# A two-layer hybrid decoder trunk on one core: the remainder of some weight slabs computed by an adding DMA in place of VectorE

## The chip, the cores and the metric

The kernel runs on one core of a Trainium2 chip. The metric is the device time of one execution in microseconds (us). Five engines matter: TensorE (PE in the profile, with PEld for its weight loads), VectorE (DVE), ScalarE (ACT), GpSimd (POOL) and SyncE (SP), which issues nearly all DMAs.

## The reference

The input, 512 tokens with 16 meta tokens ahead of them, goes through two layers of width 1024. Cut to what matters here:

```
for l in range(2):
    h = layer_norm(a * h + 0.5 * swiglu(h, ffn 0 of layer l))
    u = h @ w_in[l]                       # split into three mixers: RG-LRU, SSD, gated DeltaNet
    h = layer_norm(a * h + concat(mixers(u)) @ w_out[l])
    h = layer_norm(a * h + 0.5 * swiglu(h, ffn 1 of layer l))
```

Each SwiGLU has a gate, an up (1024x2816) and a down matrix (2816x1024). All weights and activations are f32.

## The kernel before

**Precision.** Every large product is made of three passes in a rounded f32 format (fp32r). A weight w is split into hi, which is w rounded, and lo = w - hi; the activations are split likewise. `gemm` sums hi*xhi, lo*xhi and hi*xlo.

**Slabs.** Weights come in slabs of 128x1024 elements (512 KB). `slab` (line 628) makes one ready. SP loads it into a raw tile `wr` (three buffers, `RAWS`). ScalarE rounds it into the hi half of a tile `wt` (six buffers, `TILES`). Then the remainder lo = raw - hi is computed either by GpSimd, in `PARTS` = 4 pieces of 128x256, or by VectorE in one instruction of 128x1024. The raw buffer is free once the remainder has been read out of it; the `wt` buffer is free after the last matmul of the slab.

**Streams.** The 528 tokens are two streams of 272 and 256. In the stretches before and after (the "shared" FFN parts) both streams use a slab once it is loaded. In the stretches between, the streams run apart: while one is in its mixer (long chains of small operations on all engines), the other fills TensorE with FFN work. There each slab is read by one stream alone. A slab of this kind has its fourth key `r` not None (FFN) or comes from `proj` or `out` of the mixer. Of the kernel's 484 slabs 168 are shared and 316 are read by one stream alone. `pools()` (line 648) takes POOL_SHARE = 0.7 of the latter for GpSimd. The remaining 95, and all shared slabs, take the VectorE branch. `weave` and `KNOTS` set how the two streams' units are interleaved.

**Order of the work.** Nothing is issued as it is written. A `Recorder` collects all operations with their data dependencies; `price` (line 121) gives each one a cost and, for DMAs and weight loads, a second figure `load`; `levels` computes from the end how much work hangs on each operation; `schedule` lists them engine by engine, in order of priority, and assigns the buffers; `issue` emits this order, and each engine works through its queue in order. `CHAINED` (line 44) names the tile tags for which the operation that ends the use of a buffer also inherits the urgency of the tile that will take this buffer next; before, these are the PSUM tiles `psg.g` and the weight tiles `wt.wt`. All instructions are issued from line 389, so the profile has nearly one line only, and groups are told apart by their tiles: `wr` raw slab, `wt` split slab, `g` PSUM of the large products, `c` PSUM of the mixers and norms, `acc` the residual sum, `fs`, `fh`, `ft`, `hid` FFN and convolution tiles, `d_*`, `db`, `lru`, `s_*` mixer tiles.

Of the kernel before, what the change touches and what calls it, by code (L numbers as in the profile page):

```python
# [12 lines left out]
ALU = mybir.AluOpType  # L13
# [27 lines left out]
KNOTS = ((0, 20), (18, 32), (30, 72), (59, 72), (69, 75), (72, 84), (72, 93), (82, 94), (88, 102), (89, 114), (93, 127), (95, 133), (108, 148), (108, 157), (114, 163), (117, 163), (117, 163), (117, 163), (117, 166), (132, 166))  # L41
FIRST = ("psg.g", "psc.c")
CFIRST = 1
CHAINED = ('psg.g', 'wt.wt')
WARM = 0.45
MARGIN = (20, 5, 5, 5, 0)
SPARE = dict(wr=99, db=99, lru=99, wt=99, mt=99, s2=99, g=99, c=3)
# [33 lines left out]
class Recorder:  # L81
# [39 lines left out]
    def price(self, eng, name, args, kw):  # L121

        a = [x for x in args if hasattr(x, "ap")]
        n = self.size(a[0])
        if name == "dma_start":
            b = n * a[0].ap[0][1] * 4
            return (1040 if eng == self.POOL else 475), b / 360.0
        if eng == self.PE:
            w, x = (a[1], a[2])
            fast = w.dtype == F32R  # L130
            c = (1 if fast else 2 if name == "transpose" else 4) / 2.4
            if self.region(a[0])[0] and self.size(w) <= 64:
                return self.PAIR, 55
            return self.size(x) * c + 2.5, self.size(w) * c
        wide = max(self.size(x) for x in a)
        psum = any(x.space == bass.MemoryType.PSUM for x in a)
        if eng == self.DVE:
            if name == "reciprocal":
                return 68 + 6.25 * n, 0
            if name in ("tensor_scalar", "tensor_copy", "memset") and not psum:  # L140
                return 68 + 0.52 * n, 0
            scalar = [x for x in a[1:] if self.size(x) == 1 < wide]
            return (127 if scalar else 68) + 1.042 * wide, 0
        if eng == self.ACT:
            extra = sum(93 for k in ("bias", "scale") if hasattr(kw.get(k), "ap"))
            return (51 if psum else 94) + 0.833 * wide + extra, 0
        if name in ("memset", "affine_select"):
            return 36 + 0.85 * n * (2 if name == "affine_select" else 1), 0
        return (120 + 3.33 * n if name == "tensor_copy" else 148 + 2.1 * n), 0
# [87 lines left out]
    def levels(self):  # L237
# [12 lines left out]
        for tag, sl in self.tags.items():  # L250
            tiles = [t for t in first if self.slot[t] is sl]
            if tag == "psg.g":
                for t, u in zip(tiles, tiles[1:]):
                    first[t].after.append((first[u], sum(o.cost for o in self.ops[first[t].seq:end[t].seq] if o.eng == self.PE and t in o.tiles)))
            if tag in CHAINED:
                done = sorted((end[t] for t in tiles), key=lambda op: op.seq)
# [142 lines left out]
class Trunk:  # L399
# [225 lines left out]
    def new_acc(self, u):  # L625
        self.acc[u] = self.tl(self.ap, [P, KD, 272], f"acc{u}")[:, :, :NTOK[u]]

    def slab(self, srcs, ncol, pool):

        nc = self.nc  # L630
        raw = self.tl(self.wr, [P, KD, P], "wr")[:, :, :ncol]
        t = self.tl(self.wt, [P, 2, KD, P], "wt", F32R)
        hi, lo = t[:, 0, :, :ncol], t[:, 1, :, :ncol]
        for c0, s in srcs:
            nc.sync.dma_start(raw[:, :, c0:c0 + s.shape[2]], s)
        nc.scalar.copy(hi, raw)
        if pool and self.pools():
            for k in range(0, KD, KD // PARTS):
                part = slice(k, k + KD // PARTS)
                nc.gpsimd.tensor_tensor(lo[:, part], raw[:, part], hi[:, part].bitcast(F32), ALU.subtract)  # L640
        else:
            nc.vector.tensor_tensor(lo, raw, hi.bitcast(F32), ALU.subtract)
        return hi, lo
# [999 lines left out]
```

## Time and profile before

| | us |
|---|---|
| three timed runs | 2479.98, 2482.42, 6374.14 (median 2482.42) |
| the profiled execution, whole | 2475.13 |
| its span, first to last instruction | 2472.2 |
| PE / DVE / ACT / POOL busy | 2303.2 / 1548.9 / 881.4 / 913.3 |

The time outside the span is 2.9 us. The third timed run stands far off the other two and plays no part in what follows. In the rows a window's numbers are the busy time of each engine and, in brackets, the count of its instructions; PEclk is the mean granted TensorE clock as a share of 2.4 GHz; the DMA share is that of the core's 16 DMA engines.

### The profile page before, as it was taken

Reading aid. Unit: us, or ns where it says so; the run is one execution under the profiler, and the core shown is the slowest. Engines: PE = TensorE matmul, PEld = TensorE weight load, DVE = VectorE, ACT = ScalarE, POOL = GpSimd, SP = SyncE. Lnnn points to the kernel's source line nnn. Section 1 sums busy time; section 2 is a strip of 40 time slices with the busy share of each in tenths; the row PEclk is TensorE's granted clock in tenths of the full one; section 3 lists DMA queues with packets and bytes.
Section 4 is the critical chain, followed back from the end, with each engine's and each line's share of the span. In section 5 each row is a group of like instructions: output and inputs, shape, how many; then the busy total and the mean of one; then the engine's idle time right before and its main releaser. Section 6 shows DMA issues by size and latency. Waiting matters only on the chain. (4 is left out here: it accounts for less than half of the span.)

```text
span 2472.2 us, 46955 instructions
## 1 busy us (share of the span) xinstructions
PE 2303.2 (93%) x18698; PEld 2199.2 (89%) x18698; DVE 1548.9 (63%) x3529; ACT 881.4 (36%) x1546; POOL 913.3 (37%) x1298
## 2 busy tenths in 40 slices
PE   8999998998888899999999999988889888999997
PEld 7999997886787899999999999978778778999997
DVE  6444468777877665444574444787788677654445
ACT  3222344342334354222242223533433344542222
POOL 4000566653554675000000006667365646740000
PEclk9999999897899899999999999989988879999999
DMA  5323454432341456232222334534234415653330
GB/s 147 98 78 102 125 151 148 124 86 66 100 128 46 145 163 187 95 95 86 79 76 84 97 93 145 165 111 134 62 86 124 118 34 166 179 164 91 94 95 34
DMA packets 426330, 271.98 MB, mean 110 GB/s; under 512 B 33420, under 2 KB 407920, under 8 KB 425856
## 3 DMA queue, kind: packets, MB, share of 16 engines
q1 hardware_dynamic: 425536, 268.83, 37.3%
q8 instruction: 146, 2.39, 0.4%
q0 software_dynamic: 576, 0.16, 0.1%
q14 instruction: 72, 0.59, 0.1%
HBM read 260.76 MB, written 8.19 MB: 109 GB/s over the span
## 5 line engine op out<-in xcount | busy, mean ns | idle before, releaser
L389 PE MATMUL g<-hh,wt 128*128 128x256 f32 (+1 forms) x7616 | 1073.2, 292 | 35.3 <-DVE fh L389 10.4
L389 PEld LDWEIGHTS g<-hh,wt 128*128 128x128 f32 x7616 | 995.2, 194 | 48.8 <-DVE fh L389 11.1
L389 POOL TENSOR_TENSOR wt<-wr,wt 128x256 fp32r<-128x256 f32 x884 | 699.8, 823 | 728.8 <-ACT wt L389 692.7
L389 ACT CAST wt<-wr 128x1024 fp32r<-128x1024 f32 x484 | 498.3, 1041 | 622.9 <-PE g L389 486.8
L389 PE MATMUL g<-hl,wt 128*128 128x256 f32 (+1 forms) x3808 | 568.0, 289 | 1.9 <-DVE hl L389 1.3
L389 PE MATMUL g<-hid,wt 128*128 128x256 f32 (+1 forms) x4224 | 541.8, 286 | 11.7 <-DVE acc L389 5.4
L389 PEld LDWEIGHTS g<-hid,wt 128*128 128x128 f32 x4224 | 524.0, 189 | 18.6 <-DVE acc L389 7.3
L389 PEld LDWEIGHTS g<-hl,wt 128*128 128x128 f32 x3808 | 507.0, 192 | 7.4 <-DVE hl L389 2.7
L389 DVE SCALAR_TENSOR_TENSOR acc<-g,acc 128x256 f32<-128x256 f32 (+1 forms) x608 | 255.7, 428 | 228.4 <-PE g L389 222.6
L389 DVE TENSOR_TENSOR wt<-wr,wt 128x1024 fp32r<-128x1024 f32 x263 | 339.3, 1301 | 93.0 <-ACT wt L389 91.2
L389 DVE SCALAR_TENSOR_TENSOR fs<-ft,g 128x272 f32<-128x272 f32 (+1 forms) x200 | 84.6, 424 | 176.4 <-ACT ft L389 175.6
L389 DVE TENSOR_TENSOR fh<-fs,g 128x256 f32<-128x256 f32 (+1 forms) x176 | 74.9, 426 | 173.1 <-PE g L389 172.6
L389 ACT ACTIVATE ft<-g 128x272 f32<-128x272 f32 (+1 forms) x208 | 80.8, 389 | 286.8 <-PE g L389 267.3
L389 ACT CAST hid<-fh 128x256 fp32r<-128x256 f32 (+1 forms) x176 | 71.9, 408 | 226.7 <-DVE fh L389 224.8
L389 POOL TENSOR_TENSOR ls<-ls,lq 128x256 f32<-128x256 f32 (+1 forms) x30 | 24.9, 829 | 268.8 <-ACT lq L389 268.5
L389 DVE TENSOR_TENSOR hid<-fh,hid 128x256 fp32r<-128x256 f32 (+1 forms) x176 | 87.0, 494 | 40.2 <-ACT hid L389 40.1
L389 POOL TENSOR_TENSOR wr<-wr,db 128x512 f32<-128x512 f32 x4 | 5.0, 1277 | 260.1 <-ACT wr L389 260.1
L389 DVE SCALAR_TENSOR_TENSOR fs<-fh,par,fs 128x272 f32<-128x272 f32 (+1 forms) x144 | 87.4, 609 | 20.1 <-ACT fh L389 11.3
L389 ACT ACTIVATE ft<-fs 128x272 f32<-128x272 f32 (+1 forms) x56 | 23.6, 425 | 82.1 <-DVE fs L389 77.8
L389 DVE SCALAR_TENSOR_TENSOR acc<-acc,par,c 128x256 f32<-128x256 f32 (+1 forms) x104 | 43.7, 482 | 8.7 <-PE c L389 8.7
L389 ACT ACTIVATE fs<-g,par 128x272 f32<-128x272 f32 (+1 forms) x48 | 25.1, 523 | 56.3 <-PE g L389 37.3
L389 ACT ACTIVATE lq<-acc 128x256 f32<-128x256 f32 (+1 forms) x84 | 34.6, 419 | 25.6 <-PE c L389 9.2
(306 smaller groups left out, 1741.2 us busy)
## 6 DMA issues: line engine op xcount, KB each, us to landing
wr<-in_ffn_w_gate_dram SPq DMA_DIRECT2D x120, 512.0 KB
wr<-in_ffn_w_up_dram SPq DMA_DIRECT2D x120, 512.0 KB
wr<-in_ffn_w_down_dram SPq DMA_DIRECT2D x120, 512.0 KB
wr<-in_w_in_dram SPq DMA_DIRECT2D x88, 512.0 KB
wr<-in_w_out_dram SPq DMA_DIRECT2D x32, 512.0 KB
res<-acc SPq DMA_DIRECT2D x2, 1088.0 KB
acc<-res SPq DMA_DIRECT2D x8, 272.0 KB
acc<-in_x_dram SPq DMA_DIRECT2D x4, 512.0 KB
```

The lines of the kernel that those rows point to most:

```text
L389: op.fn(*[on(x) for x in op.args], **{k: on(x) for k, x in op.kw.items()})
```

## The change

For a slab that one stream alone reads and that `pools()` does not give to GpSimd, ScalarE now writes the negated rounded weights into lo (`mul` by -1) and then hi, and a DMA issued from GpSimd's queue adds raw onto lo in place. VectorE's subtract of such a slab goes. Shared slabs and GpSimd's slabs are as before. `price` gets a cost for an adding DMA, 880 ns of its queue and twice a plain transfer's load, and `CHAINED` gets the raw tiles `wr.wr`; both enter the planned order of everything.

```diff
-CHAINED = ('psg.g', 'wt.wt')
+CHAINED = ('psg.g', 'wt.wt', 'wr.wr')
...
         if name == "dma_start":
             b = n * a[0].ap[0][1] * 4
+            if kw.get("accum_op") is not None:
+                return 880, 2 * b / 360.0
             return (1040 if eng == self.POOL else 475), b / 360.0
...
-    def slab(self, srcs, ncol, pool):
+    def slab(self, srcs, ncol, alone):
...
         for c0, s in srcs:
             nc.sync.dma_start(raw[:, :, c0:c0 + s.shape[2]], s)
+        if alone and not self.pools():
+            nc.scalar.mul(lo, raw, -1.0)
+            nc.scalar.copy(hi, raw)
+            nc.gpsimd.dma_start(lo, raw, accum_op=ALU.add)
+            return hi, lo
         nc.scalar.copy(hi, raw)
-        if pool and self.pools():
+        if alone:
             for k in range(0, KD, KD // PARTS):
                 part = slice(k, k + KD // PARTS)
                 nc.gpsimd.tensor_tensor(lo[:, part], raw[:, part], hi[:, part].bitcast(F32), ALU.subtract)
```

## Rows read from the trace of the kernel before

**Rows 1.** The page: busy time of each engine and share of the span.
```profile
PE 2303.2 (93%) x18698; PEld 2199.2 (89%) x18698; DVE 1548.9 (63%) x3529; ACT 881.4 (36%) x1546; POOL 913.3 (37%) x1298
```

**Rows 2.** Windows: two mixer stretches, two edges and a shared stretch, all instructions.
```profile
core 0: us, PE busy (x) PEld busy (x) DVE busy (x) ACT busy (x) POOL busy (x), PEclk, DMA share, GB/s
400.00:900.00 500.00, 439.43 (x3611) 397.30 (x3611) 385.37 (x1003) 204.82 (x396) 285.54 (x412) 0.90 0.37 105
900.00:1000.00 100.00, 98.14 (x796) 96.67 (x796) 52.37 (x94) 39.69 (x53) 54.60 (x71) 1.00 0.58 174
1600.00:2100.00 500.00, 434.68 (x3550) 389.71 (x3550) 372.91 (x1003) 196.78 (x385) 285.83 (x414) 0.88 0.38 107
2100.00:2180.00 80.00, 78.45 (x648) 77.14 (x646) 49.07 (x102) 39.82 (x62) 59.19 (x75) 1.00 0.56 165
...
1000.00:1500.00 500.00, 496.24 (x4027) 493.20 (x4026) 258.67 (x498) 142.63 (x242) 19.74 (x23) 1.00 0.29 87
```

**Rows 3.** Windows: the instructions on wt alone, in the two mixer stretches.
```profile
400.00:900.00 500.00, 313.77 (x2219) 292.43 (x2219) 35.29 (x28) 96.41 (x93) 210.00 (x259) 0.90 0.37 105
...
1600.00:2100.00 500.00, 302.29 (x2128) 279.92 (x2128) 35.11 (x27) 92.88 (x90) 204.86 (x252) 0.88 0.38 107
```

**Rows 4.** Groups of the whole span: the three operations that split a slab.
```profile
L389 POOL TENSOR_TENSOR wt<-wr,wt 128x256 fp32r<-128x256 f32 x884 | 699.8, 823 | 728.8 <-ACT wt L389 692.7
L389 ACT CAST wt<-wr 128x1024 fp32r<-128x1024 f32 x484 | 498.3, 1041 | 622.9 <-PE g L389 486.8
L389 DVE TENSOR_TENSOR wt<-wr,wt 128x1024 fp32r<-128x1024 f32 x263 | 339.3, 1301 | 93.0 <-ACT wt L389 91.2
```

**Rows 5.** The chain of waits, 1826 to 2088 us: shares, then three of its pieces.
```profile
by line: PE g L389 25.7%; PE c L389 20.0%; DVE fs L389 8.7%; DVE d_sq L389 5.3%; DVE l_h L389 3.9%; issue 3.3%; DVE acc L389 3.3%; DVE wt L389 2.9%; DVE db L389 2.7%; DVE d_ss L389 2.5%; DVE lru L389 2.5%; DVE d_t L389 2.0%; ACT wt L389 1.9
...
1881.66 4.29 POOL wt L389 x4
...
1928.80 1.13 DVE wt L389
...
1934.32 1.03 ACT wt L389
```

**Rows 6.** Windows: the instructions on wt alone, 1826 to 2088 us.
```profile
1826.00:2088.00 262.00, 156.68 (x1111) 146.55 (x1112) 17.11 (x13) 47.47 (x46) 106.69 (x128) 0.86 0.38 107
```

**Rows 7.** Waits of SP's queue and of ACT, 900 to 1000 us: us in total, times, longest.
```profile
SPq L389 <- POOL wt L389: 36.8, 16, 3.1
SPq L389 <- DVE wt L389: 15.8, 6, 6.8
...
ACT wt L389 <- PE g L389: 27.7, 9, 5.9
```

**Rows 8.** The chain of waits, one raw buffer's round in an edge: start, us, what.
```profile
2089.99 4.86 DMA wr<-in_ffn_w_gate_dram
...
2094.93 1.06 ACT wt L389
...
2096.06 3.13 POOL wt L389 x4
...
2156.55 3.60 DMA wr<-in_ffn_w_down_dram
```

**Rows 9.** The page: DMA queue of the loads; DMA issues on GpSimd's queue (KB, us to landing).
```profile
q1 hardware_dynamic: 425536, 268.83, 37.3%
...
fh<-in_ln_b_dram POOLq DMA_DIRECT2D x1, 24.0 KB, 6.6
...
fh<-in_ssd_dt_bias_dram POOLq DMA_DIRECT2D x1, 8.0 KB, 2.8
```

**Rows 10.** Timeline of POOL at the start: DMA issues, us each.
```profile
1.56 0.70 POOL L389 DMA_DIRECT2D fh<-in_ln_g_dram  x1
2.25 0.52 POOL L389 DMA_DIRECT2D fh<-in_ln_b_dram  x1
```

**Rows 11.** Waits of PE, 1500 to 2180 us: the three longest.
```profile
PE c L389 <- DVE db L389: 9.5, 7, 4.0
PE c L389 <- DVE lv L389: 5.6, 2, 4.9
PE c L389 <- DVE dt_g L389: 5.4, 2, 4.7
```

**Rows 12.** Tile wt on POOL, 320 to 1000 us: ns min/median/max.
```profile
L389 POOL TENSOR_TENSOR wt<-wr,wt x390: 250/741/2600, 319.0 to 973.8; 128x256 fp32r<-128x256 f32 x193, 128x32 fp32r<-128x32 f32 x2
```

## The prediction

> **What bounds the kernel now.** The page comes first: PE is busy for 93% of the span, no other engine for more than 63% [rows 1]. So time can only come out of PE's gaps and out of stretches where its clock is low, and the windows show where these are. In the shared stretch from 1000 to 1500 us PE is busy for 496 of 500 us at full clock; nothing is to be had there, and the change leaves its slabs alone. In the two mixer stretches (400 to 900 and 1600 to 2100 us) PE is busy for 439 and 435 of 500 us, so 61 + 65 = 126 us are gaps, and the mean clock is 0.90 and 0.88. Between the two levels, 1 and 0.5, that is a fifth to a quarter of the time at 1.2 GHz. DVE is at 77% and 75% there, the highest of the other engines [rows 2]. The list of PE's waits says the same: the longest are all on small DVE results of the mixers [rows 11]. Around the mixers lie four edges where one stream's FFN runs almost by itself (two stand in rows 2). There PE is at 98% and full clock, and the work that could run out is the supply of slabs: DMA share 0.56 to 0.58, and SP's queue waits most for POOL to release a raw buffer [rows 2, 7].
>
> **What goes.** 95 of the 263 DVE subtracts, each 1.30 us [rows 4]: 95 x 1.30 = 124 us of DVE. 28 + 27 = 55 of them lie in the mixer stretches [rows 3], where 55 x 1.3 = 72 us out of 758 us bring DVE from 76% to 69%. The other 40 lie in the edges, where DVE is half idle. What a subtract is worth is read from the chain of waits. From 1826 to 2088 us, 2.9% of 262 us = 7.6 us of the chain are DVE on wt [rows 5], and 13 such instructions ran there [rows 6]: 0.58 us of the 1.3 is on the chain, on average. 55 x 0.58 = 32 us. This supposes that no second chain is close behind; between nothing and the whole 72 us is possible, and I take 32, since it is read from the same stretch.
>
> **What comes, on ScalarE.** 95 multiplies of 128x1024. No such form stands in the trace; the nearest is the rounding copy of the same shape, 1.04 us [rows 4], so 99 us on an engine at 40% in the mixers. Below, it can't be shorter than nothing; above, twice the copy. I take 1.04. On the chain, ACT on wt holds 1.9% of 262 = 5.0 us for 46 copies [rows 5, 6], 0.11 us each: 55 x 0.11 = 6 us lost. (With the multiply first, hi comes 1.04 us later; the six wt buffers hide that, since ACT often waits for PE to free one of them [rows 7].)
>
> **What comes, on GpSimd's queue.** 95 DMA issues. The trace has small ones of 0.52 to 0.70 us [rows 10]; an adding one of 128 rows does not occur. I take 0.7 and, as ends, 0.5 and 3.1 (the four subtracts of a whole slab, rows 8). The queue is in order, so an issue that waits for ACT's multiply holds up the subtracts and mixer operations behind it, for up to one ACT operation of 1.04 us. POOL on wt has one piece of 4.3 us on that chain against 106.7 us busy [rows 5, 6], 4%: 55 x (0.7 + 1.04) x 4% = 4 us. The same rows count for the gain: with 32 - 6 - 4 = 22 us, the mixers get faster by 22.
>
> POOL's pieces take 0.74 us in the median and up to 2.6 [rows 12], so something on the core holds them up now and then. The Trainium skill (SBUF — State Buffer, section "Who interferes with whom") states that a VectorE instruction with two SBUF inputs blocks GpSimd's reads, and that a DMA issued from GpSimd is starved of its descriptors while VectorE runs in a two-port mode. By the first half POOL would gain where a subtract goes, by the second the new issues would stretch. No row tells these apart, and the sum holds neither.
>
> **What comes, on the DMA engines and the raw buffers.** A slab's remainder is now ready when the DMA has landed, and its raw buffer is held until then. That time is not in the trace. The loads move 268.8 MB in 37.3% of 2472 us, so 291 GB/s when all engines are busy [rows 9], and 512 KB take 1.8 us. Two reads for one write make it 3.6 at most, and the short fixed part of a DMA from GpSimd's queue is 2.8 us [rows 9]: 6.4 us from issue to landing. The ends are 3.6 us (a down slab's load, which has long rows as well, rows 8) and 6.6 + 2 x 4.86 = 16.3 us (the worst small DMA and two gate loads in a row, rows 8, 9). I take 6.4.
> The Trainium skill (Collectives: The Full Stack, "The bandwidth ceiling: the fold count and why AG ≠ RS ≠ AR") states that an add needs two source reads and so halves the rate of a copy, while the add itself costs nothing. No run here shows it; by it the data part would be the 3.6 us above.
>
> One round of a raw buffer now: load 4.86, copy 1.06, four subtracts 3.13, hand-overs 0.2, so 9.3 us with POOL [rows 8], and 4.86 + 1.06 + 1.30 + 0.2 = 7.4 with DVE. With 70% and 30%, over three buffers, a slab can come every (0.7 x 9.3 + 0.3 x 7.4) / 3 = 2.9 us. PE needs 24 matmuls per slab, 98.14 / 796 x 24 = 2.96 us [rows 2]: the supply just suffices. After the change the 30% take 4.86 + 1.06 + 0.7 + 6.4 + 0.2 = 13.2 us, and a slab comes every (0.7 x 9.3 + 0.3 x 13.2) / 3 = 3.5 us. In the mixer stretches that does no harm (500 us / 93 slabs = 5.4 us per slab, rows 3). The edges hold 316 - 183 = 133 slabs, 33 each; there 33 x 0.54 = 18 us are short, less the stock in the wt buffers (six, of which two are in use: 4 x 2.96 = 12 us). So 6 us per edge, 24 in all. The bounds are -6 us (PE's 2% of gaps over some 340 us of edges can't give more) and 4 x 18 = 72 us without stock. I take a third of the 24, 8 us, because the new CHAINED entry moves the operations that free a raw buffer forward; the trace shows no size for this.
>
> **The sum.** Against the profiled execution's 2475.1 us: -22 + 8 = -14, so 2461. The two near runs lie 5 to 7 us above that execution (2479.98 and the median 2482.42), so on the median's scale 2482.4 - 14 = 2468.
>
> **The rivals.**
> - VectorE is the bound of the mixers. Then all 72 us of subtracts come out, less 6 on ACT: 2482 - 66 = 2416. For it: DVE at 77%, PE's waits on DVE, and a clock that may rise when gaps close [rows 2, 11]. Against it: only 2.9% of the chain is DVE on wt [rows 5].
> - Nothing: the mixer's small operations form a second chain just behind, ACT and POOL take back what DVE gives, and the new order is as good as the old: 2480. For it: 'PE g' and 'PE c' hold 46% of the chain [rows 5].
> - The supply breaks in the edges, on the other side. The adding DMAs read and write what the loads' engines must carry: some 10 per 100 us x 3.6 us are 0.36 on top of a DMA share of 0.58, 0.94. If landings lengthen by a fifth (loads 5.8, adding DMAs 7.7), rounds are 10.2 and 15.5 us, a slab comes every 3.9 us, and 33 x 0.97 - 12 = 20 us are lost per edge, 80 in all: 2482 - 22 + 80 = 2540. It decides from 3.5 us per slab (18 us short, all of the mixers' gain gone), and passes 2% at 3.9. For it: supply and need are level now, 2.9 against 2.96. Against: the edges are only 30 to 35 slabs long, and the stock covers the first part.
>
> **How the numbers follow.** The forecast has 0.42, VectorE as the bound 0.24, nothing 0.11, the broken supply 0.23. Two per cent (50 us) is about what a measurement of this kernel can tell from no change. Faster by over 2%: 0.24. Within 2%: 0.42 + 0.11 = 0.53. Slower: 0.23. Cases of both signs hold weight, so the forecast's own range is 2445 to 2490; the range that holds 8 in 10 reaches from 2410 (all of DVE's 72 us) to 2535 (most of the broken supply).
>
> **What would show it.** In the profile after: 168 DVE subtracts on wt, not 263; 579 ScalarE operations on wt; 95 adding DMAs on GpSimd's queue with 0.7 us each and about 6.4 us to landing. In the mixers DVE's share falls by some seven points, PE's gaps from 126 to about 105 us. In the edges PE stays over 95%, and SP's queue waits for landings of the adding DMAs. I am wrong if landings take over 8 us and the edges' PE falls to 90%, or if PE's gaps in the mixers stay.

## The result, and the profile after

The changed kernel takes 2578.6 us (median of 4 runs) against 2481.2 us before (median of 4, of which one took 6374.14 us; without it 2479.98): a ratio of 1.0395, 95% interval 1.0357 to 1.0432. It is 4% slower, outside the forecast's range; of the rivals it is the third, the supply that breaks in the edges. The profiled execution took 2582.6 us with a span of 2580.9, so 108.7 us more than the span of before (11 us more than the medians lie apart), and these are the ones to be found.

The page of the changed kernel, engines and DMA queues (packets, MB, share of 16 engines), against [rows 1, 9]:

```profile
PE 2362.7 (92%) x18742; PEld 2234.3 (87%) x18742; DVE 1459.3 (57%) x3434; ACT 962.9 (37%) x1641; POOL 935.3 (36%) x1393
...
q1 hardware_dynamic: 425536, 268.83, 36.1%
q0 software_dynamic: 15152, 49.51, 10.8%
...
wt<-wr POOLq DMA_DIRECT2D x94, 512.0 KB, 5.2
```

The groups that split a slab, against [rows 4] (busy us, mean ns, idle before them and releaser):

```profile
L391 POOL TENSOR_TENSOR wt<-wr,wt 128x256 fp32r<-128x256 f32 x884 | 668.0, 827 | 553.4 <-ACT wt L391 507.7
...
L391 DVE TENSOR_TENSOR wt<-wr,wt 128x1024 fp32r<-128x1024 f32 x168 | 207.4, 1252 | 54.4 <-ACT wt L391 54.1
...
L391 POOL DMA_DIRECT2D wt<-wr x95 | 82.4, 867 | 273.8 <-ACT wt L391 247.9
...
L391 ACT ACTIVATE wt<-wr 128x1024 fp32r<-128x1024 f32 x95 | 99.8, 1050 | 16.0 <-PE g L391 4.6
```

Piece by piece the change does what it says: 263 - 168 = 95 subtracts are gone from DVE, 95 multiplies of 1.05 us and 95 issues of 0.87 us have come, and an adding DMA lands 5.2 us after its issue, sooner than the 6.4 us of the forecast. No single price here is far above its forecast. The loss is in how the pieces meet, and the way to see it is to cut both spans at the same events: the first and last POOL subtract on `wt` of each layer, the first small operation of a mixer (the memset of `smd`), and the last square root of the second stream's SSD norm (`s_sv`). In the changed kernel these events stand in (first and last start, for the two halves of the span):

```profile
L391 POOL TENSOR_TENSOR wt<-wr,wt x440: 247/744/1337, 251.9 to 1030.0; 128x256 fp32r<-128x256 f32 x146, 128x32 fp32r<-128x32 f32 x1
...
L391 POOL TENSOR_TENSOR wt<-wr,wt x444: 242/743/2450, 1521.9 to 2312.8; 128x256 fp32r<-128x256 f32 x144, 128x32 fp32r<-128x32 f32 x4
...
L391 POOL MEMSET smd<- x2: 194/195/196, 387.7 to 1674.8; 16x128 f32 x2
...
L391 DVE SCALAR_TENSOR_TENSOR s_sv<-s_sv x12: 146/151/693, 629.4 to 831.2; 128x6 f32<-128x6 f32 x6, 128x4 f32<-128x4 f32 x6
...
L391 DVE SCALAR_TENSOR_TENSOR s_sv<-s_sv x12: 141/150/154, 1914.0 to 2111.6; 128x6 f32<-128x6 f32 x6, 128x4 f32<-128x4 f32 x6
```

Windows of the kernel before between these events: edge 1, mixers, edge 2, edge 3, mixers, edge 4 (the second number is the length):

```profile
251.80:378.70 126.90, 124.51 (x986) 121.04 (x985) 74.69 (x149) 53.21 (x86) 80.77 (x105) 1.00 0.48 138
378.70:815.20 436.50, 379.43 (x3158) 337.58 (x3157) 343.64 (x919) 175.11 (x352) 239.19 (x369) 0.89 0.36 101
815.20:973.80 158.60, 150.79 (x1195) 148.91 (x1196) 96.50 (x204) 69.68 (x105) 112.42 (x138) 0.96 0.54 164
1471.50:1600.20 128.70, 127.46 (x1006) 125.45 (x1006) 74.00 (x151) 55.31 (x88) 77.31 (x106) 0.99 0.49 140
1600.20:2042.90 442.70, 382.11 (x3128) 338.16 (x3127) 331.31 (x915) 173.40 (x349) 246.72 (x366) 0.88 0.36 99
2042.90:2201.60 158.70, 152.00 (x1241) 149.51 (x1242) 99.33 (x209) 71.74 (x108) 112.82 (x143) 0.98 0.56 167
```

The same windows of the changed kernel:

```profile
251.90:387.70 135.80, 126.64 (x979) 122.72 (x978) 62.32 (x139) 60.71 (x94) 78.46 (x108) 0.97 0.65 166
387.70:831.20 443.50, 393.65 (x3144) 344.93 (x3142) 320.44 (x910) 193.04 (x372) 250.57 (x395) 0.87 0.51 126
831.20:1030.00 198.80, 172.32 (x1276) 165.97 (x1277) 86.06 (x179) 85.56 (x124) 114.38 (x155) 0.94 0.66 168
1521.90:1674.80 152.90, 139.85 (x1065) 133.51 (x1065) 64.88 (x145) 65.57 (x101) 83.38 (x118) 0.98 0.62 158
1674.80:2111.60 436.80, 376.23 (x3058) 330.44 (x3056) 323.63 (x901) 190.15 (x369) 250.18 (x391) 0.87 0.51 127
2111.60:2312.80 201.20, 179.62 (x1331) 170.31 (x1332) 78.88 (x189) 85.22 (x124) 112.19 (x154) 0.93 0.67 170
```

The four edges grew from 572.9 to 688.7 us, +115.8. The mixers went from 879.2 to 880.3, +1.1, although DVE has less to do there. All else, the shared stretches and both ends, fell by 8 us. So the loss is in the edges, and there DVE, the engine that was relieved, is busy for less than half of the time. In edge 4 PE falls from 96% to 89% and its mean clock from 0.98 to 0.93; the gaps bring a second loss with them, since part of the work then runs at the lower of the two levels.

The 115.8 us have three parts. PE's gaps in the edges grew from 18 to 70 us, by 52. The edges hold 4651 matmuls in place of 4428: the planned order of the changed kernel puts some 223 here that stood in other stretches, which at the 0.125 us of a matmul in the edges before (554.8 / 4428) is about 28 us of moved work and no loss. The remaining 36 us are matmuls that take longer, 0.133 us each. This is an estimate, since a few matmul records are missing from a trace (44 more stand in this one than in that of before). Taken like for like the edges lose about 88 us and the mixers, which have 84 matmuls fewer, about 12.

What holds the edges up is in the chain of waits of the changed kernel in edge 4 (2111 to 2313 us; shares, then single pieces: start, us, what):

```profile
by line: PE g L391 41.4%; issue 13.9%; POOL wt L391 13.2%; DMA wr<-in_ffn_w_down_dram 6.6%; DMA wr<-in_ffn_w_up_dram 6.6%; DMA wt<-wr 5.1%; DMA wr<-in_ffn_w_gate_dram 3.4%; ACT wt L391 3.1%; DVE d_sq L391 2.7%; PE c L391 1.8%; DVE fh L391 0
...
2184.92 6.75 DMA wr<-in_ffn_w_up_dram
2195.86 5.33 DMA wt<-wr
2223.31 6.60 DMA wr<-in_ffn_w_up_dram
2236.27 4.28 DMA wr<-in_ffn_w_down_dram
2245.88 4.94 DMA wt<-wr
2275.94 6.82 DMA wr<-in_ffn_w_gate_dram
```

About half of the chain is the making of slabs: loads, adding DMAs, POOL and ACT on `wt`, and the issue gaps between them. Two things stand in the pieces. The adding DMAs themselves are on it, 4.9 and 5.3 us each. And the loads on it are long: 6.6 to 6.8 us for gate and up slabs and 4.3 for a down slab, against 4.86 and 3.60 in [rows 8]. The chain picks out the long ones, though. Over all loads issued in the four edges, from issue to the landing signal in the trace, the median of gate and up slabs went from 3.98 to 4.68 us, of down slabs from 3.74 to 4.32, of all from 3.96 to 4.55. While the three long loads ran, the 16 DMA engines were nearly full; the means of 0.62 to 0.67 over an edge mix full stretches with empty ones:

```profile
2184.92:2191.67 6.75, 6.75 (x57) 6.57 (x56) 3.47 (x6) 3.32 (x8) 3.87 (x5) 1.00 0.95 215
2223.31:2229.91 6.60, 6.60 (x57) 6.60 (x56) 0.85 (x2) 1.45 (x3) 2.83 (x4) 1.00 0.94 225
2275.94:2282.76 6.82, 3.77 (x26) 3.57 (x25) 1.06 (x3) 1.04 (x1) 2.77 (x4) 0.86 0.94 232
```

The timeline shows one round of a slab:

```profile
2244.34 1.05 ACT L391 ACTIVATE wt<-wr 128x1024 fp32r<-128x1024 f32 x1
...
2245.88 0.86 POOL L391 DMA_DIRECT2D wt<-wr  x1
...
2250.87 7.25 PE L391 MATMUL g<-hid,wt 128*128 128x256 f32 x36 [3.75 <-DMA wt<-wr]
2250.90 0.37 SPq L391 DMA_DIRECT2D wr<-in_ffn_w_gate_dram  x1
...
2252.75 1.05 ACT L391 CAST wt<-wr 128x1024 fp32r<-128x1024 f32 x1 [5.47 <-DMA wr<-in_ffn_w_up_dram]
```

The issue at 2245.88 lands at 2250.8. Only then does PE go on, after 3.75 us without work (its granted clock is 0.50 in the 5 us that follow), and only then does SP load the next slab into the raw buffer that was set free. ACT meanwhile has stood idle for 5.47 us until an earlier load came. A buffer, a lo and a load come late together, and the trace alone does not say which of them costs what.

### The profile page after: what moved, and what is told of

It reads as the page before. It is cut to its first block, busy times and chain, and to the rows that moved or that the text cites. A ratio compares the mean times of both kernels' runs of the same rounds, so it can differ in the third digit from the quotient of the medians.

```text
span 2580.9 us, 47062 instructions
## 1 busy us (share of the span) xinstructions
PE 2362.7 (92%) x18742; PEld 2234.3 (87%) x18742; DVE 1459.3 (57%) x3434; ACT 962.9 (37%) x1641; POOL 935.3 (36%) x1393
## 3 DMA queue, kind: packets, MB, share of 16 engines
q0 software_dynamic: 15152, 49.51, 10.8%
## 5 line engine op out<-in xcount | busy, mean ns | idle before, releaser
L391 POOL TENSOR_TENSOR wt<-wr,wt 128x256 fp32r<-128x256 f32 x884 | 668.0, 827 | 553.4 <-ACT wt L391 507.7
L391 PE MATMUL g<-hid,wt 128*128 128x256 f32 (+1 forms) x4224 | 576.7, 293 | 54.3 <-DMA wt<-wr 21.0
L391 PEld LDWEIGHTS g<-hid,wt 128*128 128x128 f32 x4224 | 543.9, 194 | 73.4 <-DMA wt<-wr 23.4
L391 PEld LDWEIGHTS g<-hl,wt 128*128 128x128 f32 x3808 | 513.5, 195 | 5.3 <-DVE hl L391 1.5
L391 DVE TENSOR_TENSOR wt<-wr,wt 128x1024 fp32r<-128x1024 f32 x168 | 207.4, 1252 | 54.4 <-ACT wt L391 54.1
L391 POOL DMA_DIRECT2D wt<-wr x95 | 82.4, 867 | 273.8 <-ACT wt L391 247.9
L391 DVE TENSOR_TENSOR hid<-fh,hid 128x256 fp32r<-128x256 f32 (+1 forms) x176 | 98.3, 559 | 52.9 <-ACT hid L391 52.8
L391 ACT ACTIVATE wt<-wr 128x1024 fp32r<-128x1024 f32 x95 | 99.8, 1050 | 16.0 <-PE g L391 4.6
```

Source lines behind the costliest of these rows:

```text
L391: op.fn(*[on(x) for x in op.args], **{k: on(x) for k, x in op.kw.items()})
```

## The experiments

The kernel before was timed again in each round of runs, and took 2472.8 to 2481.8 us in them. So kernels of different rounds are compared by their ratios to it, and differences of ratios are given in us of 2480.

The first question was whether the DMA is at fault at all, or ScalarE's extra operation and the new planned order.

**Without the adding DMA.** The line of the DMA is deleted; lo stays minus the rounded weights.

```diff
-            nc.gpsimd.dma_start(lo, raw, accum_op=ALU.add)
```

> The changed kernel without the adding DMA: the 95 slabs get lo = minus the rounded weights (ScalarE) and nothing is added, so their remainder is wrong and raw is free after ScalarE's two operations. Theory A (the adding DMA itself, by holding raw buffers or by its traffic, starves the four edges): the 116 us that the edges lost come back, 2455 to 2485 us. Theory B (ScalarE's extra operation, or the new planned order with the raw tiles chained, is at fault): it stays at 2540 us or more. It also shows what VectorE's relief is worth when nothing is paid for it: by my prediction some 30 us, 2450.

Measured: 2440.6 us, ratio 0.9837 (0.9795 to 0.988), faster than the range of either theory. Theory B falls. With all of ScalarE's additional work and the same entry in `CHAINED` the kernel is 138 us faster than the changed one and 41 us faster than before; all of the loss, and more, hangs on the adding DMA. The windows between the same events show where the relief of DVE went:

```profile
252.40:377.20 124.80, 123.20 (x989) 121.39 (x988) 61.32 (x141) 63.80 (x98) 75.68 (x106) 1.00 0.50 146
377.20:799.50 422.30, 376.15 (x3112) 331.29 (x3111) 314.14 (x902) 193.31 (x371) 231.12 (x366) 0.89 0.37 102
799.50:952.90 153.40, 151.23 (x1210) 150.12 (x1211) 75.94 (x182) 83.56 (x121) 103.78 (x143) 0.98 0.58 174
1450.90:1576.10 125.20, 124.93 (x1000) 123.03 (x999) 57.51 (x140) 62.79 (x95) 74.93 (x106) 1.00 0.51 145
1576.10:2004.80 428.70, 375.23 (x3121) 329.99 (x3119) 303.86 (x892) 192.59 (x374) 231.90 (x363) 0.89 0.37 102
2004.80:2168.00 163.20, 156.77 (x1262) 154.66 (x1263) 85.18 (x197) 86.73 (x123) 106.22 (x144) 0.97 0.54 162
```

The mixers take 422.3 + 428.7 = 851.0 us, 28 less than before and 21 less than with the new order alone (871.9, below); the edges take 566.6, which is no difference that can be read. The gain that was forecast for the mixers, 26 us without the DMA issues, is there, and the adding DMA takes it back. What this run doesn't tell is whether it is the adding: a plain copy of the same bytes from GpSimd's queue was not run.

**The order alone, and the DMA alone.** Two halves of the change: the new `CHAINED` on the kernel before, and the changed kernel with the old `CHAINED`.

```diff
# order_only: the kernel before
-CHAINED = ('psg.g', 'wt.wt')
+CHAINED = ('psg.g', 'wt.wt', 'wr.wr')
# dma_only: the changed kernel
-CHAINED = ('psg.g', 'wt.wt', 'wr.wr')
+CHAINED = ('psg.g', 'wt.wt')
```

> The kernel before with the raw tiles added to CHAINED, and no adding DMA. Theory B (order): slower by 2% or more, 2530 us and up. Theory A: within 1% of the kernel before, 2460 to 2505 us.

> The changed kernel with CHAINED as before (no raw tiles in it). If the new entry in the order is at fault (theory B), near 2480 us. If the adding DMA is at fault whatever the order, 2560 to 2620 us.

Measured: the order alone 2467.6 us, ratio 0.9949 (0.9925 to 0.9973), a small gain; the DMA alone 2602.3 us, ratio 1.0492 (1.0432 to 1.0552). Both lie in the ranges given for the adding DMA as the cause. The new order helps in both kernels, by half a per cent and by a full one. It is not the cause, and the slowdown of the DMA is even larger than the result of the two together.

**Adding from hi.** To part the held raw buffer from the rest, the DMA reads hi, already in the `wt` tile, in place of raw. Bytes, rows and number stay; lo comes out as zero.

```diff
-            nc.gpsimd.dma_start(lo, raw, accum_op=ALU.add)
+            nc.gpsimd.dma_start(lo, hi, accum_op=ALU.add)
```

> The adding DMA reads the rounded weights hi in place of raw: same 95 DMAs, rows and bytes, but the remainder comes out as zero and raw is free after ScalarE's copy. Theory A1 (the raw buffer held until the landing is what starves the edges): near the kernel before, 2500 us or less. Theory A2 (the DMAs' traffic on the shared DMA engines, or a late lo): within 25 us of the changed kernel, 2555 us or more.

Measured: 2539.7 us, ratio 1.0239 (1.0182 to 1.0297), between the two expectations. Raw held until the landing is part of it: 39 us of the whole time. In the edges alone it is 71 us (688.7 against 617.8), of which some 29 are matmuls that stand in other stretches here (4423 in the edges against 4651), so about 42 like for like. The DMA lands later here than in the changed kernel, 7.2 us after its issue in place of 5.2. If TensorE loses more by a late lo for that, which the mixers' 904.9 us against 880.3 would fit but no run shows by itself, the 39 us are a lower estimate.

**Nobody waits for lo.** The matmuls of these slabs read hi twice.

```diff
-            nc.gpsimd.dma_start(lo, raw, accum_op=ALU.add)
-            return hi, lo
+            nc.gpsimd.dma_start(lo, hi, accum_op=ALU.add)
+            return hi, hi
```

> As add_from_hi, but the matmuls of the 95 slabs read hi in place of lo as well (wrong products), so nothing but the reuse of the buffer waits for the landings. Theory C (the DMAs' traffic, 49 MB more through the engines that carry the loads, makes the loads late): within 20 us of add_from_hi, 2520 to 2560 us. Theory D (TensorE waits for a lo that lands late): 2440 to 2475 us, near the kernel without the adding DMA.

Measured: 2506.6 us, ratio 1.0137 (1.0093 to 1.0182), again between the two. By the ratios the wait for lo costs 25 us. The mixers' time falls from 904.9 to 876.5 us, while the edges stay at 617.9, with 130 more matmuls in them; so the wait is paid in the mixers at least, and the edges can't be cleared of it. What is left, 74 us over the kernel without the DMA, is paid although nothing waits for a landing but the reuse of a buffer.

**An eighth of the bytes.** Twice: with raw held and lo waited for (`tiny_add`), and from hi with nobody waiting (`tiny_side`).

```diff
# tiny_add: an eighth of raw; lo is awaited
+            nc.gpsimd.dma_start(lo[:, :1], raw[:, :1], accum_op=ALU.add)
+            return hi, lo
# tiny_side: an eighth of hi; nobody waits
+            nc.gpsimd.dma_start(lo[:, :1], hi[:, :1], accum_op=ALU.add)
+            return hi, hi
```

> The changed kernel, adding only the first eighth of each slab (64 KB in place of 512; the remainder of the rest is wrong): 95 issues, waits and landings as before, an eighth of the traffic. Theory C (bytes): 2440 to 2480 us. Theory E (fixed cost of each adding DMA: issue on GpSimd's queue, its wait for ScalarE, the way to the landing with raw held so long): 2520 us or more.

> As side_add, but each adding DMA takes only the first eighth of hi (64 KB): the raw buffer is not held, nobody waits for lo (the matmuls read hi twice, wrong products), the traffic is an eighth. What is left over the kernel without the adding DMA is the issue in GpSimd's in-order queue. In side_add the four edges take 618 us, without the DMA 567. Theory C (bytes on the DMA engines): edges 565 to 585 us here, whole time 2445 to 2470. Theory E (GpSimd's queue: 0.87 us per issue and the wait for ScalarE): edges 600 us or more, whole time 2485 or more.

Measured: 2491.5 us, ratio 1.0077 (1.0034 to 1.0119), and 2468.5 us, ratio 0.9975 (0.9943 to 1.0007). The first lies between its two ranges; the second lies in theory C's range by its time and 4 us above it by its edges. So neither the bytes nor what comes with every DMA is the whole. The issues on GpSimd's queue, with the eighth of the bytes that goes with them, cost 34 us by the ratios (the edges 588.9 against 566.6). The other seven eighths of the bytes, which nobody waits for, cost 40 us, and with raw held and lo awaited 79 us. The loads follow the bytes: their median in the edges is 3.98 and 4.05 us with an eighth, 4.59 and 4.61 with all of them read from hi, 3.96 without the DMA. The page of `tiny_add` shows that a short transfer lands in 2.7 us:

```profile
q1 hardware_dynamic: 425536, 268.83, 37.5%
q0 software_dynamic: 14256, 6.33, 2.2%
...
wt<-wr POOLq DMA_DIRECT2D x94, 64.0 KB, 2.7
```

**A fourth raw buffer.** It fits only if other buffers go, so a control with the same buffers and no adding DMA was run later.

```diff
-RAWS = 3
+RAWS = 4
-MT_BUFS = 3
-S2_BUFS = 5
+MT_BUFS = 2
+S2_BUFS = 4
```

> The changed kernel with four raw buffers, paid for by one buffer less of mt (3 to 2) and of s2 (5 to 4). If three raw buffers starve the edges, a fourth gives back most of the edges' 116 us: 2470 to 2520 us, unless the mixers lose by their buffers. If the DMA engines are the limit, it stays at 2550 us or more.

> Control of raws4: the kernel before with the raw tiles chained, four raw buffers, mt 2 and s2 4, no adding DMA. If the smaller mt and s2 are what raws4 lost in the mixers (53 us), the mixers take 910 to 940 us here in place of 872; the edges stay at 555 to 570 us, since three raw buffers were enough without the adding DMA. If four raw buffers help here too, the edges fall below 550.

Measured: 2573.9 us, ratio 1.041 (1.0341 to 1.0478), and the control 2493.9 us, ratio 1.006 (1.0028 to 1.0092). By the whole time the fourth buffer brings nothing. By the windows the edges fall from 688.7 to 632.6 us, 56 of their 116 (some 43 like for like, with 105 matmuls fewer), while the mixers rise from 880.3 to 933.0. In the control the mixers take 897.5 us in place of 871.9, so the smaller mt and s2 explain about half of that rise; the other half stays open. The control's edges, 569.7 us, show that three raw buffers are enough without the adding DMA.

**The DMA in the mixers alone.** Slabs of the mixers' projections keep the adding DMA (35 of them), the FFN slabs go back to VectorE.

```diff
-        if alone and not self.pools():
+        pool = alone and self.pools()
+        if alone == 2 and not pool:
...
-            self.specs[key] = (srcs, c, True)
+            self.specs[key] = (srcs, c, 2)
```

> Adding DMA only for slabs of the mixers' projections (some 37 of the 95); FFN slabs read by one stream go back to VectorE, raw tiles chained. The edges are then as before; the mixers gain VectorE time but get the traffic. If the edges alone are the cost: 2445 to 2470 us, at or below the kernel with only the order changed (2468). If the traffic costs as much in the mixers as the relief brings there: 2465 to 2500 us.

Measured: 2491.9 us, ratio 1.0077 (1.0046 to 1.0109). This is the second expectation. The edges are nearly whole again, 575.7 us, but the mixers take 887.2, against 871.9 with the order alone, and the whole is 32 us slower by the ratios. In the mixers too the DMA costs more than the relief brings.

**The split between GpSimd and VectorE.** DVE's relief without a DMA, and its opposite, on the kernel before with the raw tiles chained.

```diff
-POOL_SHARE = 0.7
+POOL_SHARE = 0.75        # order_share65: 0.65
```

> The kernel before with the raw tiles chained and 75% in place of 70% of the one-stream slabs on GpSimd: 16 subtracts fewer on VectorE without any DMA. If VectorE's relief is worth what the kernel without the adding DMA showed (28 us of mixers for 95 slabs), some 3 to 5 us under the kernel with the order alone: 2460 to 2466. If GpSimd's 3 us per slab starve the edges: 2470 to 2500 us.

> The kernel before with the raw tiles chained and 65% of the one-stream slabs on GpSimd: 16 slabs more on VectorE, whose round of a raw buffer is 7.4 us in place of 9.3. With 75% both the edges (594 against 564 us) and the mixers (918 against 872) got slower. If GpSimd's share is what binds the edges, 65% is at or below 70%: 2450 to 2470 us. If VectorE's time in the mixers binds, 2475 to 2500 us.

Measured: 2520.8 us, ratio 1.0178 (1.0116 to 1.0241), and 2477.7 us, ratio 1.0001 (0.9977 to 1.0024). Both expectations of the first missed; it is slower than either said, in the edges (593.9 us) and in the mixers (918.2) alike. The second came out in the range that was given for a bound by VectorE in the mixers, but there it takes 876.4 us against 871.9, so that reason isn't shown; its edges take 577.5. Neither beats the order alone, which is the fastest complete kernel here.

The times of the stages in one table (us; one profiled execution each, and each kernel has a planned order of its own, so differences under some 10 us are not read; the count of matmuls tells how much work stands in the edges):

| kernel | edges | matmuls in them | mixers | ratio to before |
|---|---|---|---|---|
| before | 572.9 | 4428 | 879.2 | 1 |
| order alone | 563.5 | 4357 | 871.9 | 0.9949 |
| without the adding DMA | 566.6 | 4461 | 851.0 | 0.9837 |
| an eighth from hi, nobody waits | 588.9 | 4494 | 856.7 | 0.9975 |
| from hi, nobody waits | 617.9 | 4553 | 876.5 | 1.0137 |
| from hi, lo awaited | 617.8 | 4423 | 904.9 | 1.0239 |
| changed kernel | 688.7 | 4651 | 880.3 | 1.0395 |
| changed, old order | 679.6 | 4602 | 906.1 | 1.0492 |
| changed, four raw buffers | 632.6 | 4546 | 933.0 | 1.041 |
| an eighth of raw, lo awaited | 609.0 | 4515 | 865.0 | 1.0077 |

## Why the prediction was wrong

**The gain in the mixers was sized right, and then taken back.** 32 us were forecast for DVE's subtracts, less 6 for ACT and 4 for POOL: 22. Without the adding DMA the mixers gain 21 over the order alone and 28 over before, with ACT's multiplies included and no issue on POOL, for which the sum has 26. So the chain was read well: the share of an operation on it, per instruction, times the number that goes. With the DMA the mixers gain nothing, since they pay for its issues, its traffic and the late lo. Only the issues had a place in the sum (4 us; the table has 6, which is below what it can tell). The sentence "in the mixer stretches that does no harm" looked at the mean supply alone, 5.4 us per slab, and left out that a lo which comes late is waited for even so: 25 us, by the step from lo awaited to nobody waiting. PE's gaps in the mixers, which were to fall from 126 to about 105 us, went from 118 to 110 between the events, and the time stayed.

**The term that failed is the edges: +8 us forecast, +116 measured, of which about 88 like for like.** Its single prices were near: landing 5.2 us against 6.4, issue 0.87 against 0.7, multiply 1.05 against 1.04. Three steps were wrong. (The forecast's edges are those between fixed times, with 133 slabs; between the events they hold 167.)

- The stock was counted as 12 us per edge, 48 in all, free to be eaten. The edges grew by 9, 40, 24 and 42 us, so what the stock covered, if anything, was gone early. Without the stock the forecast's own formula gives its upper bound of 72 us.
- The 24 us that were left were cut to 8 for the new entry in `CHAINED`, without a row. The entry does help, by 24 us in the changed kernel (2578.6 against 2602.3), but not at this place: with it the edges take 688.7 us and without it 679.6. What it shortens are the mixers, 880.3 against 906.1.
- The loads' own time was kept as it was. It became longer by 0.6 to 0.7 us in the median (gate and up slabs 3.98 to 4.68), and by 2 us in the pieces on the chain. The adding DMAs carry 49.5 MB at 10.8% of the engines' span; less the 0.1% that the parameter loads take, that is 0.107 x 2581 / 95 = 2.9 us of all 16 engines each, and the DMA share of the edges rose from between 0.48 and 0.56 to between 0.62 and 0.67. This was the mechanism of the third rival, which put the engines at 0.94 and the loads at 5.8. While the long loads ran the engines were at 0.94 and 0.95, as it said; over a whole edge they were not, and the typical load lengthened less. The Trainium skill (Collectives: The Full Stack, "The bandwidth ceiling: the fold count and why AG ≠ RS ≠ AR") has an add at half a copy's rate, because it reads two sources. The 2.9 us are 1.6 times the 1.8 us of a load, but most loads move in packets of 512 bytes and the adding DMA in packets of 4 KB; among packets of 4 KB the trace has 362 ns on average against 200 of the loads, 1.8 times (medians 338 and 159, 2.1 times), so it bears the page out.

Put into the forecast's own formula, the measured times do not give the whole loss. Two of three FFN slabs are gate or up (4.68 us) and one is down (4.32), 4.56 us on average. The round of an adding slab is then 4.56 + 1.06 + 0.87 + 5.2 + 0.2 = 11.9 us, that of a POOL slab 4.56 + 1.06 + 3.13 + 0.2 = 8.95, and a slab comes every (0.7 x 8.95 + 0.3 x 11.9) / 3 = 3.3 us, an estimate. Measured: from 2200 to 2300 us PE ran 600 matmuls on `wt`, 25 slabs, 4.0 us each. So the formula gives a third of the step from the 2.96 us that PE needs to the 4.0 that it got. (The forecast's 4.86 us for a load was a long one too: with it the formula gave 2.9 and 3.5, and with the median loads of before, 3.9 us, it gives 2.6 for before.) The formula adds up the steps and has no term for a slab's waits between them: in edge 4 POOL stood idle for 79.3 us until ScalarE had written `wt`, against 38.1 before. Which of these waits makes the rest is open.

**What the runs show of the causes, in order.** From the kernel without the DMA to the changed one, 138 us by the ratios: 34 for the issues on GpSimd's queue with an eighth of the bytes, 40 for the bytes that nobody waits for, 25 for TensorE waiting for lo, 39 for raw held until the landing. The intervals of the ratios leave each of them open by some 15 us. In the edges alone it is 22, 29, 0 and 71, and like for like, with the moved matmuls taken out, about 18, 22, 16 and 42; so there the raw buffer is the main thing, and the fourth buffer, which takes 56 us from the edges (43 like for like), says the same. The last two steps run through a kernel whose DMAs land 2 us later than in the changed one; the line between them is therefore not sharp, and their sum of 64 us is the safer number. Why the issues cost 34 us, by their own 0.87 us or by what waits behind them in GpSimd's queue, was not tried.

**The other signs.** The counts of instructions came as forecast (168, 579, 95). GpSimd's subtracts are no shorter with 95 of DVE's gone (827 ns against 823), so the gain for POOL that the forecast left out of its sum doesn't show here. Without the adding DMA it does: 785 ns, against 826 with the order alone. The new issues took 0.86 us in the median and at most 1.56; what stretched a few of them isn't shown. DVE's share in the mixers fell by 4 points (from 77% to 73%), not seven. Of the signs of being wrong, landings over 8 us with PE at 90% in the edges, the second came (618.4 of 688.7 us are 90%) without the first. SP's queue did wait for adding DMAs, 22.9 us in 11 waits in edge 4, but more for POOL, 96.5 us in 32: the adding DMA delays the loads, and what shows as a wait is whoever is last:

```profile
SPq L391 <- POOL wt L391: 96.5, 32, 6.5
SPq L391 <- ACT wt L391: 57.6, 18, 6.4
SPq L391 <- DMA wt<-wr: 22.9, 11, 4.8
```

## What to carry to other kernels

Work that is taken from an engine and given to a DMA isn't priced by its duration alone: it holds its source buffer until the landing, it lengthens the other transfers of the stretch, and its issue sits in an in-order queue. Price it in the stretch with the least slack in its supply, not in the one where the relieved engine is busy; here the gain was 21 to 28 us in the mixers and the bill 116 us in the edges, about 88 of them like for like. And read a typical duration from all transfers of a stretch: those on the chain of waits are the long ones. Where a ring of buffers feeds the bound engine and supply and need are level, put the longer transfers into the round before trusting a stock, and try the deletion of the new operation first: it shows at once what the relief is worth.

## What the runs showed of the hardware

- Loads of 512 KB in the edges took 4.55 us in the median beside adding DMAs of 512 KB, against 3.96 before and 4.05 beside adding DMAs of 64 KB. The three of 6.6 to 6.8 us on the chain ran while the DMA engines were busy for 94 to 95% of the time.
- An adding DMA of 512 KB from one SBUF tile to another took 2.9 us of all 16 engines and landed in 5.2 us; one of 64 KB in 2.7 us. Read from the fp32r half of the tile that it adds to, in place of the raw f32 tile, the same sizes landed in 7.2 and 4.9 us. Of the 2 us about 1.4 lie before the first packet moves (2.9 us after the issue in place of 1.4, medians of the 512 KB DMAs); why is not shown.
- Sixteen more slabs on GpSimd (75% in place of 70%) cost 57 us over the order alone by the ratios, more than half of what 95 adding DMAs cost over the kernel before (97 us); why the split is that steep stays open.
